# Moving the quarter sums of the last down-projection from GpSimd to VectorE

## The chip, the cores and the metric

The kernel runs on one core of a Trainium2 chip. The metric is device time in microseconds (us) of one execution. A core has TensorE (PE: matrix products; loading a weight tile is shown as PEld), VectorE (DVE), ScalarE (ACT), GpSimd (POOL) and SyncE (SP, whose queue issues all DMAs here). Each engine works through its own instructions in order and waits on semaphores for the others.

## The reference, cut to what matters

One layer of a transformer-like trunk over 1024 latent tokens with 256 context tokens, all in float32 and `D_MODEL = 1024`, `D_FF = 2816`: a half-weighted SwiGLU feed-forward, two kinds of attention merged by gates, and a second half-weighted SwiGLU feed-forward. The change lies in the second feed-forward, the last of the layer:

```python
def _swiglu(h, w1, w3, w2):
    return (jax.nn.silu(h @ w1) * (h @ w3)) @ w2
...
        x = _residual(x, _swiglu(_modnorm(x, g[4], m[6], m[7]), ffn2_w1[l], ffn2_w3[l], ffn2_w2[l]),
                      g[5], m[8], HALF_STEP)
```

`_residual` normalises the rows of its second argument, scales them by `g[5]` and the adaLN gate `m[8]`, and adds them to `x`.

## The kernel before

**Products.** Every float32 matrix is split into a high part that TensorE takes exactly and a low part, the remainder. `split` (line 202) does it: ScalarE copies the source to the high part with rounding, VectorE subtracts the high part from the source for the low part. Three matmuls per tile (high x high, high x low, low x high) give the product (`mm3`; all matmuls are recorded at line 153). Calls on VectorE, ScalarE and GpSimd that go through a helper show line 120, DMAs of SP's queue line 132.

**Seven products instead of eight.** Both projections of the feed-forward cut their matrices into 2 x 2 quarters and use a Strassen-Winograd scheme: seven products of quarters or of sums of quarters. The sums are made ahead of the products.

**Up-projection.** `units2` holds 22 units, two for each of the NP = 11 pairs of feature tiles: one for `w1`, one for `w3`. A unit's products are steps of 12 matmuls; the steps that remain in this stage are named p6, p5, p7, p3, p4 (units that were begun earlier, 14 of the 22) or first, p6, second, p5, p7, p3, p4. Each step's result is read out of its PSUM bank by VectorE. When p4 of a pair's `w3` unit is out, the four gated quarters a11, a12, a21, a22 of that pair (128 x 512 each) are complete, and `Gated.sums` (line 719) makes from them s1 = a21 + a22, s3 = a11 - a21, s2 = s1 - a11 and s4 = a12 - s2, on GpSimd, all four at that point. They go to DRAM; `store` puts a DMA off by a number of steps (4 here). For the pairs begun early, a11 comes back from DRAM beforehand.

**Last stage.** `Quarters` (line 804) is the down-projection: 7 x 11 = 77 steps, numbered 0 to 76, seven quarter products of 11 steps each in the order of `ORDER`:

```python
        ORDER = (("a11", "b11"), ("a12", "b21"), ("s1", "t1"), ("s4", "b22"), ("s2", "t2"), ("s3", "t3"), ("a22", "t4"))
        BANKS = (("s", "s", "s", "m"), ("m", "m", "v", "v"))
```

The left factors are read back from DRAM (`load_a`), the right ones are quarters b11 ... b22 of the weight `ffn2_w2` (`load_b`) or their differences t1 = b12 - b11, t2 = b22 - t1, t3 = b22 - b12, t4 = b21 - t2. `Quarters.sum` (line 842) makes those in place, per pair, on GpSimd: 44 in all. A step multiplies four row tiles into four PSUM banks; after the last step of a quarter product, `out` (line 873) adds the banks to the result `ys`, on ScalarE for the first two products (steps 10 and 21) and on VectorE after that (steps 32, 43, 54, 65, 76). Products 0 and 1, 2 and 3, and 4 to 6 go on accumulating in the same banks, so steps 11, 33, 55 and 66 wait until the banks have been read.

**The order around it.** `Plan` is a list of main steps (TensorE's work with what reads it) and, by step, of side work; `run` records, per step, the main function, its side work in the order in which it was planned, and then the stores that are due. So each engine's order is written out by hand. `Quarters.plan` (line 889) places the left factor's load 7 steps ahead of its use, both splits 3 steps ahead, b11 and b21 7 steps ahead of theirs, b12 from step -1 on, b22 from step 14 on (one pair per step each), and the sums of pair p at steps 9 + p (t1), 26 + p (t2 and t3) and 37 + p (t4). In a step, the split comes ahead of a sum.

Two other things share the stage. The rows of adaLN modulation 8 are computed by VectorE in steps 12 to 38: 16 multiply-adds of 128 x 512 (`ada_steps`, line 2236), and some small matmuls on TensorE. And `done2` (line 2196) makes the residual of row tiles 0 to 3 in steps 55 to 62: a load of `x` and a multiplication in one step, a multiply-add of 128 x 1024 and the store of the output in the next; the last four row tiles follow in halves at the end. Splits, sums and results use the buffer pools "t" (20 of 128 x 512), "u" (24 of 128 x 1024) and "v" (16 of 128 x 1024).

Of the kernel before, what the change touches and what calls it, by code (L numbers as in the profile page):

```python
# [12 lines left out]
ALU = mybir.AluOpType  # L13
# [17 lines left out]
NP = NF // 2  # L31
# [12 lines left out]
def hybrid_block(ctx: ExitStack, tc: tile.TileContext, a: dict, out: bass.AP):  # L44
# [31 lines left out]
    def T2(dt=F32, n=512):  # L76
        return pools["t"].tile([P, n], dt, tag="t", name=nm("t"))
# [10 lines left out]
    def PB(tag):  # L88
        return ps.tile([P, 512], F32, tag=tag, name=nm("b" + tag), bufs=PBUFS[tag])
# [41 lines left out]
    def put(dst, src):  # L131
        return pin(nc.sync.dma_start(dst, src))  # L132

    def store(dst, src, n=2):

        if clock[0] is None:
            return put(dst, src)
        waiting.append((clock[0] + n, dst, src))

    def flush(before=None):  # L140
        while waiting and (before is None or waiting[0][0] <= before):
            put(*waiting.pop(0)[1:])

    deferred = []

    def later(f):
# [3 lines left out]
    vec, act, pool = Engine(nc.vector), Engine(nc.scalar), Engine(nc.gpsimd)  # L150
# [12 lines left out]
    class Plan:  # L163
# [14 lines left out]
        def run(self):  # L178
            for i, f in enumerate(self.main):
                clock[0] = i  # L180
                f()
                for g in self.side.pop(i, ()):
                    g()
                while deferred:
                    deferred.pop(0)()
                flush(i)
            assert not self.side
            clock[0] = None
            flush()
# [229 lines left out]
    class Planes:  # L419
# [52 lines left out]
        def sums(self):  # L472
            def parts(name, src):
                us = self.us[name] = [[], []]

                def one(x):
                    for hl in range(2):
                        us[hl].append(U(F32R, "u" if (name, x, hl) == self.keys.get("u") else self.keys[name]))
                    split_to(us[0][x], us[1][x], src()[x])
                    if x:  # L480
                        self.f[name] = [[half(us[hl], k) for hl in range(2)] for k in range(4)]
                return [lambda x=x: one(x) for x in range(2)]

            t11, t12, t21, t22 = [lambda o=o, s=s: getattr(self, s)[o:o + 2] for s, o in
                                  (("t1", 0), ("t1", 2), ("t2", 0), ("t2", 2))]

            def op(eng, out, x, y, o):
                return [lambda i=i: eng.tensor_tensor(out()[i], x()[i], y()[i], op=o) for i in range(2)]

            return (op(vec, t22, t22, t21, ALU.add) + parts("s1", t22) + op(vec, t21, t11, t21, ALU.subtract)  # L490
                    + op(vec, t22, t22, t11, ALU.subtract) + parts("s2", t22)
                    + op(vec, t12, t12, t22, ALU.subtract) + parts("s3", t21) + parts("s4", t12))

    class Unit:
# [32 lines left out]
        def sum(self, i):  # L527

            if i == 1:
                self.t = []  # L530
            q = {f"{r}{c}": self.r[c - 1][:, (r - 1) * 512:r * 512] for r in (1, 2) for c in (1, 2)}
            x, y = {1: ("12", "11"), 2: ("22", 0), 3: ("22", "12"), 4: ("21", 1)}[i]
            t = T2()
            vec.tensor_tensor(t, q[x], q[y] if isinstance(y, str) else self.t[y], op=ALU.subtract)
            self.t.append(t)
# [86 lines left out]
    def plan_leads(plan, units, n, ahead=0):  # L622

        at = len(plan.main)
        for x in range(0, n, 2):
            two = units[x:x + 2]
            o = at + 2 * x
            if x > ahead:
                plan.spread([lambda u=u: u.load(0) for u in two], max(at, o - 8), max(at, o - 8) + 2)
                plan.spread([lambda u=u, n=n: u.split(n) for n in ("11", "21") for u in two], o - 4, o)  # L630
        plan.step(*lead_main(units[:n]))

    def plan_rest(plan, units):

        for i, u in enumerate(units):
            o = len(plan.main)
            e = plan.step(*u.rest())
            at = lambda n: o + u.names.index(n)
            for n, f in (u.within() if i else []) + (units[i + 1].before() if i + 1 < len(units) else []):
                plan.spread([f], at(n), at(n) + 1)  # L640
            if i + 2 < len(units):
                plan.spread([lambda v=units[i + 2], x=x: v.load(x) for x in (2, 0, 1)], e - 3, e)

    def plan_first_rest(plan, units, early, first, last):
        plan.spread([lambda x=x: units[0].load(x) for x in range(2)], early, early + 1)
        plan.spread([lambda i=i: units[0].sum(i) for i in range(1, 5)], early + 2, early + 4)
        plan.spread(units[0].all_steps(), first, last)
        plan.spread([lambda: units[0].load(2)] + [lambda x=x: units[1].load(x) for x in (2, 0, 1)], last - 2, last)
# [51 lines left out]
    class Gated:  # L700
# [18 lines left out]
        def sums(self, p):  # L719
            a11, a12, a21, a22 = [self.t.pop(n) for n in ("a11", "a12", "a21", "a22")]  # L720
            s1, s4 = T2(), T2()
            pool.tensor_tensor(s1, a21, a22, op=ALU.add)
            pool.tensor_tensor(a21, a11, a21, op=ALU.subtract)
            pool.tensor_tensor(a11, s1, a11, op=ALU.subtract)
            pool.tensor_tensor(s4, a12, a11, op=ALU.subtract)
            for n, x in (("s1", s1), ("s3", a21), ("s2", a11), ("s4", s4)):
                store(self.d[n, p], x, 4)

    def up_units(h, w1, w3, gd):

# [73 lines left out]
    class Quarters:  # L804
# [37 lines left out]
        def sum(self, name, p):  # L842
            out, x, y = {"t1": ("t1", "b12", "b11"), "t3": ("t3", "b22", "b12"),
                         "t2": ("t2", "b22", "t1"), "t4": ("t4", "b21", "t2")}[name]
            pool.tensor_tensor(self.slot(out, p), self.slot(x, p), self.slot(y, p), op=ALU.subtract)

        def banks(self, x):
            self.pb = [PB(t) for t in self.BANKS[x]]
# [40 lines left out]
        def plan(self, plan, ahead=3, loads=4):  # L889

            o = len(plan.main)
            at = lambda n: o + n
            for n in range(self.n):
                plan.spread([lambda n=n: self.load_a(n)], at(n) - ahead - loads, at(n) - ahead - loads + 1)
                x = min(at(n) - ahead, at(self.n - self.LAST) - 1)
                plan.spread([lambda n=n: self.split(n)], x, x + 1)
                plan.step(lambda n=n: self.step(n))
            for p in range(NP):
                for name, first in (("b11", 0), ("b21", NP), ("b12", 6), ("b22", NP + 10)):
                    x = at(first + p) - ahead - loads  # L900
                    plan.spread([lambda name=name, p=p: self.load_b(name, p)], x, x + 1)
                for name, x in (("t1", NP - 2 + p), ("t3", 2 * NP + 4 + p), ("t2", 2 * NP + 4 + p), ("t4", 3 * NP + 4 + p)):
                    plan.spread([lambda name=name, p=p: self.sum(name, p)], at(x), at(x) + 1)
            return o

# [45 lines left out]
    first = [PB("s") for _ in range(3)]  # L951
# [211 lines left out]
    for i, d in enumerate(downs):  # L1163
# [6 lines left out]
        else:  # L1170
            order = ([None] * 4 + list(range(10)) if i == len(downs) - 2 else
                     [0, 1, 2, 3, 4, None, 5, None, 6, None, 7, None, None, 8, 9])
            for t in order:
                if t is None:
                    f, x = ups.pop(0)
# [8 lines left out]
        if i < len(downs) - 2:  # L1184
            n = downs[i + 1]
            plan.spread([lambda n=n: n.loads(n.fs[0])], o, o + 1)
            plan.spread(n.steps(), o + 3, e)
        elif not last:
            n = downs[i + 1]
# [78 lines left out]
    def emit_cq(i, ci, x, bank):  # L1268

        t, q = x, T2()  # L1270
        if bank:
            t = T2()
            act.copy(t, x)
        act.activation(q, t, AF.Square)
        if ci in sq:
            vec.tensor_tensor(sq[ci], sq[ci], q, op=ALU.add)
        else:
            sq[ci] = q
        store(cqx[i, :, ci * 512:(ci + 1) * 512], t)
# [22 lines left out]
    for p in range(3):  # L1302
        punits.append(Unit(h2, [cq_src(2 * p), cq_src(2 * p + 1)],
                           lambda i, ci, x, bank, p=p: emit_cq(2 * p + i, ci, x, bank)))
# [227 lines left out]
    def tiles_of(ci):  # L1532
        return range(CHUNKS[ci][0] // P, sum(CHUNKS[ci]) // P)
# [199 lines left out]
    def head_out(pv, n, h, hi, lo, shape):  # L1733
# [20 lines left out]
        nc.gpsimd.tensor_tensor(lo[b:b + 64], o, f32(hi[b:b + 64]), op=ALU.subtract)  # L1754

    sums, held = {}, [None]

    def wide(n):
# [384 lines left out]
    def chain2(t):  # L2143
        made = []

        def run(x):
            if not made:
                made.extend(residual_steps(y2[t], x1s[t * P:(t + 1) * P, :], lambda: g5row[0], True, ready[t // 4],
                                           after=lambda: store(x2s[t * P:(t + 1) * P, :], y2[t], 1)))
            made[x]()  # L2150
        return [lambda x=x: run(x) for x in range(5)]
# [177 lines left out]
```

## Time and profile before

| | us |
|---|---|
| median of 3 runs | 2626.81 |
| lowest, highest | 2623.81, 2628.51 |
| the profiled execution | 2623.75 |
| its span in the profile | 2622.0 |
| TensorE busy | 2577.2 (98%) |
| VectorE busy | 1891.3 (72%) |
| ScalarE busy | 1190.2 (45%) |
| GpSimd busy | 371.9 (14%) |

How to read it: the profile is one execution, taken by the hardware profiler. A row of a group gives line, engine, operation, output<-inputs by the program's names (xu, xv and t are tiles of the pools u, v, t; bs, bm, bv are PSUM banks; d is a tensor in DRAM), the tile's shape, the count, then busy time in us and the mean of one in ns, and last how long the engine sat idle before such instructions and what ended that. In the timeline a row is start, duration, engine and operation, with the wait before it in brackets; rows of equal kind in a run are merged (x9). Matmuls are pipelined and their ends are modelled, so intervals between starts are used for TensorE. "PEclk" is the clock that TensorE was granted, as a share of full speed. GpSimd's spans are rough.

### The profile page before, as it was taken

Reading aid. Unit: us, or ns where it says so; the run is one execution under the profiler, and the core shown is the slowest. Engines: PE = TensorE matmul, PEld = TensorE weight load, DVE = VectorE, ACT = ScalarE, POOL = GpSimd, SP = SyncE. Lnnn points to the kernel's source line nnn. Section 1 sums busy time; section 2 is a strip of 40 time slices with the busy share of each in tenths; the row PEclk is TensorE's granted clock in tenths of the full one; section 3 lists DMA queues with packets and bytes.
Section 4 is the critical chain, followed back from the end, with each engine's and each line's share of the span. In section 5 each row is a group of like instructions: output and inputs, shape, how many; then the busy total and the mean of one; then the engine's idle time right before and its main releaser. Section 6 shows DMA issues by size and latency. Waiting matters only on the chain. (4 is left out here: it accounts for less than half of the span.)

```text
span 2622.0 us, 38011 instructions
## 1 busy us (share of the span) xinstructions
PE 2577.2 (98%) x13596; PEld 2191.1 (84%) x13596; DVE 1891.3 (72%) x3448; ACT 1190.2 (45%) x2282; POOL 371.9 (14%) x456
## 2 busy tenths in 40 slices
PE   8999999999999999999999999999999999999898
PEld 6888888888888788889889999987788888888687
DVE  4778876588776676774469988887545788778867
ACT  6622233522223763433438988772265322324344
POOL 1000000000000400001004422220030121114613
PEclk9999999999999999999999999999999999999999
DMA  8444433444433665745978722216235454238414
GB/s 307 164 157 144 149 110 123 158 162 157 158 135 105 219 235 185 241 149 180 299 287 294 221 75 76 68 49 217 84 131 170 165 176 146 100 117 302 162 58 173
DMA packets 213501, 433.30 MB, mean 165 GB/s; under 512 B 26880, under 2 KB 68032, under 8 KB 213312
## 3 DMA queue, kind: packets, MB, share of 16 engines
q1 hardware_dynamic: 213312, 430.87, 49.1%
q8 instruction: 107, 1.75, 0.3%
q14 instruction: 82, 0.67, 0.1%
HBM read 318.78 MB, written 112.00 MB: 164 GB/s over the span
## 5 line engine op out<-in xcount | busy, mean ns | idle before, releaser
L153 PE MATMUL bm<-xu,xu 128*128 128x512 f32 (+1 forms) x1980 | 469.6, 388 | 0.6 <-DVE xu L120 0.3
L153 PEld LDWEIGHTS bm<-xu,xu 128*128 128x128 f32 x1980 | 363.4, 188 | 73.9 <-ACT t L120 1.4
L153 PE MATMUL bs<-xv,xu 128*128 128x512 f32 x1488 | 357.3, 389 | 0.3 <-DVE t L120 0.3
L153 PE MATMUL bv<-xv,xu 128*128 128x512 f32 x1342 | 335.4, 389 | 0.0
L153 PE MATMUL bs<-xu,xu 128*128 128x512 f32 (+1 forms) x1404 | 334.0, 384 | 0.0
L153 PEld LDWEIGHTS bs<-xv,xu 128*128 128x128 f32 x1488 | 279.2, 188 | 58.5 <-issue 0.7
L120 ACT CAST xu<-t 128x512 fp32r<-128x512 f32 x260 | 158.4, 616 | 352.6 <-DVE t L120 352.1
L153 PEld LDWEIGHTS bs<-xu,xu 128*128 128x128 f32 x1404 | 258.0, 188 | 52.0 <-issue 0.8
L153 PEld LDWEIGHTS bv<-xv,xu 128*128 128x128 f32 x1342 | 251.9, 188 | 52.3
L120 DVE TENSOR_TENSOR xu<-t,xu 128x512 fp32r<-128x512 f32 x260 | 181.6, 700 | 127.5 <-ACT xu L120 127.5
L120 POOL TENSOR_SCALAR st<-st 128x1 f32<-128x1 f32 (+1 forms) x66 | 42.6, 646 | 1413.2 <-ACT t L120 1402.8
L120 DVE TENSOR_TENSOR xu<-xu,xu 128x512 fp32r<-128x512 f32 (+1 forms) x212 | 161.3, 766 | 65.9 <-ACT xu L120 65.5
L153 PE MATMUL bs<-w,w 96*128 96x512 f32 (+3 forms) x832 | 206.4, 367 | 2.4 <-DVE st L1798 2.0
L120 DVE TENSOR_TENSOR xu<-xv,xu 128x512 fp32r<-128x512 f32 (+4 forms) x196 | 141.4, 744 | 42.0 <-ACT xu L120 38.8
L153 PE MATMUL bm<-t,xu 128*128 128x256 f32 (+1 forms) x1272 | 165.3, 287 | 0.6 <-ACT t L120 0.4
L153 PEld LDWEIGHTS bm<-t,xu 128*128 128x128 f32 x1272 | 160.7, 191 | 6.0 <-ACT t L120 0.8
L120 ACT ACTIVATE t<-t 128x512 f32<-128x512 f32 (+1 forms) x94 | 57.3, 610 | 226.7 <-DVE t L120 211.7
L153 PE MATMUL bv<-t,w 128*128 128x256 f32 x896 | 151.5, 288 | 2.8 <-DVE t L1936 2.0
L153 PEld LDWEIGHTS bv<-t,w 128*128 128x128 f32 x896 | 132.8, 189 | 18.6 <-DVE t L1936 6.9
L120 ACT CAST xu<-xu 128x512 fp32r<-128x512 f32 (+1 forms) x212 | 130.2, 624 | 14.9 <-DMA xu<-in_f1w 7.8
L153 PEld LDWEIGHTS bs<-w,w 96*128 96x128 f32 (+1 forms) x832 | 123.6, 190 | 10.8 <-DVE st L1798 3.5
L1936 DVE TENSOR_TENSOR t<-bm,t 128x512 fp32r<-128x512 f32 x160 | 110.0, 688 | 27.7 <-ACT t L1935 27.2
(227 smaller groups left out, 4304.6 us busy)
## 6 DMA issues: line engine op xcount, KB each, us to landing
d<-t SPq DMA_DIRECT2D x305, 256.0 KB, 2.7
t<-d SPq DMA_DIRECT2D x160, 256.0 KB, 3.8
xv<-in_f1w SPq DMA_DIRECT2D x64, 512.0 KB, 3.6
xu<-in_f1w SPq DMA_DIRECT2D x61, 512.0 KB, 3.8
xu<-in_f2w SPq DMA_DIRECT2D x58, 512.0 KB, 3.7
t<-in_wada SPq DMA_DIRECT2D x112, 256.0 KB, 3.9
xv<-d SPq DMA_DIRECT2D x40, 512.0 KB, 6.0
xu<-in_winT SPq DMA_DIRECT2D x38, 512.0 KB, 4.8
```

Source lines behind the costliest of these rows:

```text
L120: return lambda *x, **y: pin(f(*x, **y))
L153: return pin(nc.tensor.matmul(o, s, m, start=start, stop=stop, skip_group_check=open_group[0]))
L1936: nc.vector.tensor_tensor(t[1], pb, f32(t[0]), op=ALU.subtract)
```

## The change

`Plan.run` gets a list `owed` and, at the end of each step's side work, runs one entry of it. `Gated.sums` puts its four sums there, each with its store, on VectorE: s1 in the step of p4, the others in the three steps after it, and each store two steps after its sum. `Quarters.sum` runs on VectorE. In `Quarters.plan` b12 is loaded three steps later and b22 five steps later, and the sums of pair p stand at steps 4 + 3p/2 (t1), 23 + 3p/2 (t2), 40 + p (t3) and 52 + p (t4), rounded down. The operands, results and number of all operations and DMAs stay.

```diff
+    owed = []
     deferred = []
...
                 while deferred:
                     deferred.pop(0)()
+                if owed:
+                    owed.pop(0)()
                 flush(i)
...
             a11, a12, a21, a22 = [self.t.pop(n) for n in ("a11", "a12", "a21", "a22")]
             s1, s4 = T2(), T2()
-            pool.tensor_tensor(s1, a21, a22, op=ALU.add)
-            pool.tensor_tensor(a21, a11, a21, op=ALU.subtract)
-            pool.tensor_tensor(a11, s1, a11, op=ALU.subtract)
-            pool.tensor_tensor(s4, a12, a11, op=ALU.subtract)
-            for n, x in (("s1", s1), ("s3", a21), ("s2", a11), ("s4", s4)):
-                store(self.d[n, p], x, 4)
+
+            def one(name, out, x, y, op):
+                vec.tensor_tensor(out, x, y, op=op)
+                store(self.d[name, p], out)
+
+            for x in (("s1", s1, a21, a22, ALU.add), ("s3", a21, a11, a21, ALU.subtract),
+                      ("s2", a11, s1, a11, ALU.subtract), ("s4", s4, a12, a11, ALU.subtract)):
+                owed.append(lambda x=x: one(*x))
...
-            pool.tensor_tensor(self.slot(out, p), self.slot(x, p), self.slot(y, p), op=ALU.subtract)
+            vec.tensor_tensor(self.slot(out, p), self.slot(x, p), self.slot(y, p), op=ALU.subtract)
...
-                for name, first in (("b11", 0), ("b21", NP), ("b12", 6), ("b22", NP + 10)):
+                for name, first in (("b11", 0), ("b21", NP), ("b12", 9), ("b22", 2 * NP + 4)):
                     x = at(first + p) - ahead - loads
                     plan.spread([lambda name=name, p=p: self.load_b(name, p)], x, x + 1)
-                for name, x in (("t1", NP - 2 + p), ("t3", 2 * NP + 4 + p), ("t2", 2 * NP + 4 + p), ("t4", 3 * NP + 4 + p)):
+                for name, x in (("t1", 4 + 3 * p // 2), ("t2", 2 * NP + 1 + 3 * p // 2), ("t3", 4 * NP - 4 + p), ("t4", 5 * NP - 3 + p)):
                     plan.spread([lambda name=name, p=p: self.sum(name, p)], at(x), at(x) + 1)
```

## The prediction

> **What bounds the kernel now.** I read the page's busy shares by slice, then busy time in windows cut at the last two stages, then who TensorE waits for, then its timeline.
>
> ```profile
> span 2622.0 us, 38011 instructions
> ...
> PE   8999999999999999999999999999999999999898
> ...
> POOL 1000000000000400001004422220030121114613
> ```
>
> A slice is 65.6 us. TensorE is full nearly everywhere; the slice from 2425 to 2491 is one of the few at 8, and there GpSimd shows a 6.
>
> ```profile
> core 0: us, PE busy (x) PEld busy (x) DVE busy (x) ACT busy (x) POOL busy (x), PEclk, DMA share, GB/s
> 2047.40:2383.40 336.00, 336.00 (x1484) 278.29 (x1484) 251.96 (x352) 103.30 (x181) 63.52 (x40) 1.00 0.41 139
> ...
> 2458.60:2489.80 31.20, 18.33 (x73) 12.86 (x72) 31.20 (x24) 7.96 (x14) 27.43 (x17) 0.96 0.37 110
> 2489.80:2506.60 16.80, 16.76 (x71) 13.10 (x72) 15.03 (x18) 4.58 (x8) 10.21 (x7) 0.87 0.50 146
> 2506.60:2583.60 77.00, 77.00 (x345) 63.66 (x343) 48.51 (x71) 38.40 (x68) 7.23 (x8) 1.00 0.25 87
> 2583.60:2614.90 31.30, 30.32 (x133) 24.70 (x132) 22.83 (x37) 13.41 (x31) 12.48 (x7) 1.00 0.39 145
> ```
>
> The up-projection (2047 to 2383) has no idle TensorE. In the middle of the last stage VectorE is busy without a gap (31.20 of 31.20 us), GpSimd nearly so, and TensorE works 18.33 us. Once GpSimd's sums are done, VectorE falls to 48.51 of 77 us and TensorE is full. So TensorE sets the time, except where VectorE does:
>
> ```profile
> PE bm L153 <- DVE xv L120: 12.9, 7, 6.9
> PE bs L153 <- DVE xv L120: 1.9, 4, 1.0
> ```
>
> In the last two stages TensorE waits for nothing but VectorE's low halves and additions (xv). The loss itself comes from TensorE's timeline:
>
> ```profile
> 2383.36 2.20 PE L153 MATMUL bs<-xv,xv 128*128 128x512 f32 x9
> ...
> 2458.64 0.39 PE L153 MATMUL bm<-xv,xv 128*128 128x512 f32 x1
> ...
> 2489.84 2.90 PE L153 MATMUL bm<-xv,xv 128*128 128x512 f32 x6 [6.89 <-DVE xv L120]
> ...
> 2506.56 1.52 PE L153 MATMUL bm<-xv,xv 128*128 128x512 f32 x6
> ...
> 2578.18 2.20 PE L153 MATMUL bs<-xv,xv 128*128 128x512 f32 x9
> ...
> 2580.90 2.20 PE L153 MATMUL bs<-xv,xv 128*128 128x512 f32 x9
> ...
> 2584.76 2.29 PE L153 MATMUL bs<-xv,xv 128*128 128x512 f32 x9 [0.98 <-DVE xv L120]
> ...
> 2612.05 2.88 PE L153 MATMUL bm<-xv,xv 128*128 128x512 f32 x12
> ```
>
> A step of 12 matmuls takes 2580.90 - 2578.18 = 2.72 us undisturbed, so 77 steps need 209.4. They ran from 2383.36 to 2612.05 + 2.88 = 2614.93: 231.6. Of the 22.1 us between, about 2 are small matmuls that stay (8 + 8 + 2 of them):
>
> ```profile
> L156 PE MATMUL bs<-ident,st 128*128 128x128 f32 x8 | 1.0, 272 | 0.0
> L153 PE MATMUL bs<-t,strip 128*32 128x256 f32 x8 | 0.6, 391 | 0.0
> L156 PE MATMUL bs<-ident,t 128*128 128x128 f32 x2 | 0.4, 272 | 0.0
> ```
>
> The losses, by step numbers of the last stage: before step 27 (due 2383.36 + 27 x 2.72 = 2456.80, there at 2458.64) 1.84; from there to step 33 (2489.84) 31.20 - 6 x 2.72 = 14.88; to step 38 (2506.56) 16.72 - 13.60 = 3.12, of which 1.0 is small matmuls: 2.1; to step 66 (2584.76) 78.20 - 76.16 = 2.04, less 1.0: about 1.1. Together 20 us.
>
> **The change part by part.** *The 44 sums leave GpSimd.* The reason for the stall is in VectorE's groups, first between 2383.4 and 2506.6, then between 2506.6 and 2583.6, where GpSimd has no sums:
>
> ```profile
> L120 DVE TENSOR_TENSOR xv<-xu,xv 128x512 fp32r<-128x512 f32 x40 | 53.4, 1336 | 0.0
> L120 DVE TENSOR_TENSOR xv<-t,xv 128x512 fp32r<-128x512 f32 x39 | 45.4, 1165 | 12.4 <-ACT xv L120 12.4
> ...
> L120 DVE TENSOR_TENSOR xv<-t,xv 128x512 fp32r<-128x512 f32 x27 | 18.6, 689 | 19.9 <-ACT xv L120 19.9
> L120 DVE TENSOR_TENSOR xv<-xu,xv 128x512 fp32r<-128x512 f32 x27 | 18.5, 686 | 0.0
> L120 DVE SCALAR_TENSOR_TENSOR xu<-xu,st,xu 128x1024 f32<-128x1024 f32 x4 | 5.1, 1285 | 6.6 <-DMA xu<-d 6.6
> ```
>
> One and the same subtraction averages 1165 to 1336 ns beside GpSimd's sums and 686 to 689 ns without. The single ones:
>
> ```profile
> 2459.78 0.74 DVE L120 SCALAR_TENSOR_TENSOR t<-t,sc,t 128x512 f32<-128x512 f32 x1
> 2460.44 1.78 DVE L120 TENSOR_TENSOR xv<-t,xv 128x512 fp32r<-128x512 f32 x1
> 2462.14 1.77 DVE L120 TENSOR_TENSOR xv<-xu,xv 128x512 fp32r<-128x512 f32 x1
> 2463.83 0.74 DVE L120 SCALAR_TENSOR_TENSOR t<-t,sc,t 128x512 f32<-128x512 f32 x1
> ```
>
> Two subtractions at 1.77 and an adaLN multiply-add make a cycle of 2463.83 - 2459.78 = 4.05 us, against TensorE's 2.72: 1.33 lost per step over some six steps, then step 33, which first needs the additions of step 32 out of its banks. Without GpSimd the cycle is 2 x 0.69 + 0.74 = 2.12 us, and a sum at 0.69 makes 2.81; but there are two sums in three steps here (t1, t2) and 16 adaLN operations in 26 steps, so a mean of 1.38 + 0.46 + 0.46 = 2.30 us. That fits into 2.72, and the splits stand three steps ahead. So 14.88 and the 2.1 behind it go. For the first 1.84 the bounds are 0 and 1.84: the splits are faster, but the loads of these steps are tight, too. I take 0.5, since the waits were for VectorE.
>
> *The price on VectorE.* 44 x 0.69 = 30 us in the last stage, behind each step's split and hidden as above. If that cover is gone they cost up to 30 us, a sum at a time.
>
> *Four sums per pair in the up-projection.* The same trade, from VectorE's groups between 2047.4 and 2383.4 and GpSimd's until 2506.6:
>
> ```profile
> L120 DVE TENSOR_TENSOR xu<-xu,xu 128x512 fp32r<-128x512 f32 x37 | 40.7, 1100 | 0.0
> L120 DVE TENSOR_TENSOR t<-xu,t 128x512 f32<-128x512 f32 x42 | 33.8, 806 | 0.0
> L120 DVE TENSOR_TENSOR t<-xu,xu 128x512 f32<-128x512 f32 x21 | 20.9, 997 | 0.0
> ...
> L120 POOL TENSOR_TENSOR t<-t,t 128x512 f32<-128x512 f32 x44 | 70.0, 1591 | 354.3 <-DVE t L120 217.0 <-ACT xu L120 113.6 <-issue 21.1
> L120 POOL TENSOR_TENSOR xu<-xu,xu 128x512 f32<-128x512 f32 x33 | 54.7, 1683 | 32.4 <-DVE xv L120 27.9 <-DMA xu<-in_f2w 4.5
> ```
>
> At 0.69 each these three groups would be 37 x 0.41 + 42 x 0.12 + 21 x 0.31 = 27 us shorter; 44 new sums are 30. VectorE's load stays (251.96 of 336 us), one sum per step instead of stalls in lumps, and each split is made two steps (5.4 us) ahead. Cost 0; bounds 0 and 30 us, all sums on the path.
>
> *New waits on VectorE.* Its queue is in order: behind a sum stand the next step's splits, and TensorE waits for those. t1 of pair 0 comes two steps after its load of b12, t2 four after b22; GpSimd waited 4.5 us for such a load in all. Two steps plus the three of the splits are 13.6 us of cover: cost 0, upper bound 4.5. SP's stores of the last pair's sums stand at steps 1 to 4 instead of 3, each holding the loads queued behind it until VectorE has that sum; s4 comes after four splits and three sums, about 12 x 0.69 = 8.3 us after the up-projection's end, the time that GpSimd needed for four sums (4 x 1.59 = 6.4) plus 2: inside the 0.5. Bytes and DMA count stay; b12 and b22 are loaded three and five steps later, which spreads the start. ScalarE and TensorE keep their order.
>
> *What is late next.* Steps 54 to 62 also hold the residuals of the first four row tiles, and t4 now comes there, one per step:
>
> ```profile
> 2559.25 1.28 DVE L120 SCALAR_TENSOR_TENSOR xu<-xu,st,xu 128x1024 f32<-128x1024 f32 x1
> 2566.11 1.29 DVE L120 SCALAR_TENSOR_TENSOR xu<-xu,st,xu 128x1024 f32<-128x1024 f32 x1 [2.03 <-DMA xu<-d]
> ...
> 2580.32 1.29 DVE L120 SCALAR_TENSOR_TENSOR xu<-xu,st,xu 128x1024 f32<-128x1024 f32 x1 [2.58 <-DMA xu<-d]
> 2583.93 1.88 DVE L120 TENSOR_TENSOR xv<-xv,bs 128x512 f32<-128x512 f32 x3
> ```
>
> These four form a chain: the store of one holds SP's next residual load, for which the next one waits; some 7 us a turn, against 5.44 for two steps. At its end the additions of step 65 are late, and step 66 waits for their banks. Two sums more per turn (1.4) fit into the 2.0 to 2.6 us that VectorE sits waiting. But three (t4 of pairs 2 to 4) come ahead of the first link, which no wait hides: 3 x 0.69 = 2.1. The 1.1 before step 66 becomes 3.2.
>
> The rule that bears on 3.2: the Trainium skill, "TensorE: Matmul & The Clock Gate" (Why this matters for your kernels), warns of TensorE gaps over about 3 us, after which it runs at half clock. The trace agrees for the gap of 6.89: six matmuls in 2.90 us instead of 1.52, clock 0.87. By the rule a gap of 3.2 would be paid again; it is a rival below.
>
> The Trainium skill's "Perfetto Trace Analysis" (Optimizing Scalar/DVE Operations) says that offloading from a saturated VectorE even to GpSimd may make sense, but adds that they share an SBUF read port. The first half speaks against this change, and by it the last stage would grow by up to 30 us; the rows (1.77 beside GpSimd, 0.69 without) bear out the second half.
>
> *Sum.* 20 - 0.5 - 3.2 = 16.5 us. The profiled execution took 2623.75 (1.75 around its span), 3.06 less than the median of 2626.81: 2607.2 against its own time, 2610.3 against the median. What the measurement can tell from no change is 0.2%, 5.3 us.
>
> **The rivals.**
> 1. *Step 66's gap costs clock, too.* After the long gap steps 33 to 37 lost 2.1; the same again gives 2612.4. For it: 3.2 lies just above the rule's bound. Against: the gap of 0.98 left the clock at 1.00 (last window above).
> 2. *Two thirds of the gain: the sums wait for loads or the tight start stays.* VectorE inherits GpSimd's 4.5 us behind b12 and the 1.84 stays, in front of splits with no lead left: 16.5 - 4.5 - 1.3 = 10.7 gained, 2616.
> 3. *It does nothing:* 1.77 us is not GpSimd's doing (DMA, ScalarE), or VectorE stays the pace through the added sums. 2627. Against: VectorE's rate turns exactly when GpSimd ends.
> 4. *Slower: the up-projection breaks.* A sum there waits on VectorE for a late a11 reload or for a buffer that a store still reads; what it holds up are TensorE's bank readouts. It decides once such a wait exceeds the two steps of lead, 5.44 us; then a pair loses about the sums' own 4 x 0.69 = 2.8 us, 11 pairs 30 us: 2610 + 30 = 2640. Against: GpSimd's group shows no DMA wait for these operands, and TensorE had no gap in 336 us although VectorE suffered lumps of about the same size.
>
> **How the numbers follow.** Forecast 0.63 (own range 2606.6, no gap at all, to 2613), rival 1 0.10, rival 2 0.15, rival 3 0.06, rival 4 0.06. Range 2603 to 2617: below by the 3 us that executions before differ among themselves, above past rivals 1 and 2. It leaves out rivals 3 and 4 and some of 2. Faster 0.88, same 0.06, slower 0.06.
>
> **What would show it.** Right: in the last stage VectorE's subtractions all at 0.69; steps 27 to 38 at 2.72 with clock 1.00; the wait before step 33 gone and the one before step 66 near 3 us; VectorE's total busy time about unchanged; GpSimd's sums gone from its groups. Wrong: gaps of TensorE in the up-projection, VectorE waiting for loads of in_f2w, or matmul steps longer than 2.72 with 0.69 us subtractions.

## The result and the profile after

| | median, us | lowest to highest | runs |
|---|---|---|---|
| before, same chip | 2627.07 | 2623.81 to 2628.51 | 4 |
| changed | 2612.03 | 2609.17 to 2613.24 | 4 |

The ratio is 0.9943, with a 95% interval from 0.9926 to 0.9960: faster by 15.0 us, where 16.5 were forecast. The profiled execution took 2611.61 us. In the changed kernel the recorded lines stand one lower, so matmuls show L154; in variants of the kernel before they show L153.

First the page of the changed kernel: span, busy time by engine, and the slices of TensorE and GpSimd.

```profile
span 2609.8 us, 37912 instructions
...
PE 2576.4 (99%) x13596; PEld 2194.1 (84%) x13596; DVE 1869.2 (72%) x3536; ACT 1189.7 (46%) x2282; POOL 229.4 (9%) x368
...
PE   8999999999999999999999999999999999999998
...
POOL 1000000000000400001003522221021000000003
```

The slice that stood at 8 (2425 to 2491 us) is a 9, and GpSimd has nothing to do there. GpSimd lost 371.9 - 229.4 = 142.5 us. VectorE took over its 88 sums and is nevertheless busy 22 us less than the 1891.3 of before. The same windows as before, for the changed kernel:

```profile
2047.40:2383.40 336.00, 336.00 (x1484) 278.19 (x1484) 245.68 (x390) 102.55 (x180) 0.00 (x0) 1.00 0.42 139
2383.40:2458.60 75.20, 75.20 (x333) 62.28 (x332) 54.51 (x90) 30.69 (x54) 0.00 (x0) 1.00 0.89 320
2458.60:2489.80 31.20, 31.20 (x144) 25.22 (x143) 26.01 (x44) 12.57 (x22) 0.00 (x0) 1.00 0.56 166
2489.80:2506.60 16.80, 16.80 (x80) 13.99 (x79) 9.57 (x17) 7.83 (x14) 0.00 (x0) 1.00 0.34 104
2506.60:2583.60 77.00, 73.97 (x320) 60.74 (x319) 66.50 (x101) 38.43 (x72) 18.72 (x12) 0.98 0.33 120
```

In the third row TensorE (second number) was busy 18.33 us and is now full, while VectorE (fourth) does its splits and its sums in 26.01 of 31.20 us where it had no pause before. The clock of 0.96 and 0.87 in the third and fourth windows is 1.00. In the last window it is the other way: TensorE, full before, loses 3.03 us, and the clock reads 0.98. TensorE's timeline of the changed kernel (start, duration) shows the only place:

```profile
2386.31 2.20 PE L154 MATMUL bs<-xv,xv 128*128 128x512 f32 x9
...
2565.05 2.23 PE L154 MATMUL bs<-xv,xv 128*128 128x512 f32 x9
2567.12 0.84 PE L154 MATMUL bm<-xv,xv 128*128 128x512 f32 x3
2570.99 3.06 PE L154 MATMUL bs<-xv,xv 128*128 128x512 f32 x9 [3.03 <-DVE xv L120]
...
2578.14 2.20 PE L154 MATMUL bs<-xv,xv 128*128 128x512 f32 x9
...
2599.90 2.88 PE L154 MATMUL bm<-xv,xv 128*128 128x512 f32 x12
```

Step 0 starts at 2386.31 and step 65 at 2565.05: 178.74 us, of which 65 x 2.72 = 176.80 are steps and the rest is the 2 us of small matmuls. So nothing is lost for 65 steps. Step 66 was due at 2565.05 + 2.72 = 2567.77 and comes 3.22 us late. Then the two steps 66 and 67 take 2578.14 - 2570.99 = 7.15 us instead of 5.44: nine matmuls last 3.06 instead of 2.20, so the clock was down, at a cost of 1.71 us. The whole stage takes 2599.90 + 2.88 - 2386.31 = 216.47 us, against 231.57 before: 15.1 shorter, which is the whole gain of 15.0. (The profiled execution came into the last stage 2.95 us later than that of before, out of stages that the change doesn't touch. There its clock fell to half twice, for 3.41 us each time, and that of before not at all; the last section shows one such place. In the runs whose up-projection has no gap of TensorE, the stage begins at 2383.4 to 2383.7 us with no such stretch ahead of it, at 2384.9 to 2385.3 with one, at 2385.2 to 2386.3 with two and at 2388.2 with three. So variants are compared by the length of this stage as well as by their times.)

VectorE's timeline of the changed kernel, first in the stretch that lost most before, then along the residual chain ahead of step 66: the additions of product 4, the four residuals, the additions of step 65.

```profile
2460.60 0.69 DVE L120 TENSOR_TENSOR xv<-t,xv 128x512 fp32r<-128x512 f32 x1
2461.21 0.69 DVE L120 TENSOR_TENSOR xv<-xu,xv 128x512 fp32r<-128x512 f32 x1
2461.82 0.69 DVE L120 TENSOR_TENSOR xu<-xu,xu 128x512 f32<-128x512 f32 x1
2462.42 0.75 DVE L120 SCALAR_TENSOR_TENSOR t<-t,sc,t 128x512 f32<-128x512 f32 x1
2463.33 0.69 DVE L120 TENSOR_TENSOR xv<-t,xv 128x512 fp32r<-128x512 f32 x1 [0.16 <-ACT xv L120]
...
2536.01 2.05 DVE L120 TENSOR_TENSOR xv<-xv,bs 128x512 f32<-128x512 f32 x3 [0.85 <-PE bs L154]
...
2545.21 1.28 DVE L120 SCALAR_TENSOR_TENSOR xu<-xu,st,xu 128x1024 f32<-128x1024 f32 x1
...
2552.17 1.28 DVE L120 SCALAR_TENSOR_TENSOR xu<-xu,st,xu 128x1024 f32<-128x1024 f32 x1 [0.94 <-DMA xu<-d]
...
2559.62 1.28 DVE L120 SCALAR_TENSOR_TENSOR xu<-xu,st,xu 128x1024 f32<-128x1024 f32 x1 [1.40 <-DMA xu<-d]
...
2566.55 1.28 DVE L120 SCALAR_TENSOR_TENSOR xu<-xu,st,xu 128x1024 f32<-128x1024 f32 x1 [0.89 <-DMA xu<-d]
...
2570.16 1.88 DVE L120 TENSOR_TENSOR xv<-xv,bs 128x512 f32<-128x512 f32 x3
```

The two splits of a step, a sum of the weight and an adaLN multiply-add stand in 2.73 us (2463.33, the next split, less 2460.60). Before, the two splits and the multiply-add alone took 4.05.

In the chain the turns are still about 7 us (6.96, 7.45, 6.93). The waits in them have shrunk from 2.0 to 2.6 us to 0.9 to 1.4: two sums a turn went into them. The last additions begin at 2570.16, 2.4 us after step 66 was due.

### The profile page after: what moved, and what is told of

Read it like the earlier page. It is cut to its first block, busy times and chain, and to the rows that moved or that the text cites. A ratio compares the mean times of both kernels' runs of the same rounds, so it can differ in the third digit from the quotient of the medians.

```text
span 2609.8 us, 37912 instructions
## 1 busy us (share of the span) xinstructions
PE 2576.4 (99%) x13596; PEld 2194.1 (84%) x13596; DVE 1869.2 (72%) x3536; ACT 1189.7 (46%) x2282; POOL 229.4 (9%) x368
## 4 chain that ended last, share of the span: by engine, by line
PE 55%; issue 32%; DVE 6%; ACT 4%; DMA 1%; POOL 1%; SPq 0%; DVEq 0%; ACTq 0%; POOLq 0%
PE bs L154 24%; PE bm L154 16%; PE bv L154 12%; PE bm L157 2%; ACT xu L1914 1%; DVE xu L1778 1%; DVE xv L120 1%; DVE t L1941 1%; ACT t L1940 1%; DVE xu L120 1%; PE bs L157 1%; DVE t L120 1%; POOL st L120 1%; ACT t L1914 0%; ACT t L1754 0%
## 5 line engine op out<-in xcount | busy, mean ns | idle before, releaser
L154 PE MATMUL bm<-xu,xu 128*128 128x512 f32 (+1 forms) x1980 | 469.6, 388 | 1.1 <-ACT t L120 0.8
L154 PEld LDWEIGHTS bm<-xu,xu 128*128 128x128 f32 x1980 | 363.4, 188 | 74.5 <-ACT t L120 2.1
L154 PE MATMUL bs<-xv,xu 128*128 128x512 f32 x1488 | 357.3, 389 | 0.3 <-DVE t L120 0.3
L154 PE MATMUL bv<-xv,xu 128*128 128x512 f32 x1342 | 335.4, 389 | 0.0
L154 PE MATMUL bs<-xu,xu 128*128 128x512 f32 (+1 forms) x1404 | 334.0, 384 | 0.0
L154 PEld LDWEIGHTS bs<-xv,xu 128*128 128x128 f32 x1488 | 279.2, 188 | 58.5 <-issue 0.7
L154 PEld LDWEIGHTS bs<-xu,xu 128*128 128x128 f32 x1404 | 258.0, 188 | 52.0 <-issue 0.8
L154 PEld LDWEIGHTS bv<-xv,xu 128*128 128x128 f32 x1342 | 251.9, 188 | 52.3
L120 DVE TENSOR_TENSOR xu<-xu,xu 128x512 fp32r<-128x512 f32 (+2 forms) x245 | 168.5, 692 | 66.2 <-ACT xu L120 64.6
L154 PE MATMUL bs<-w,w 96*128 96x512 f32 (+3 forms) x832 | 206.8, 367 | 2.4 <-DVE st L1803 1.9
L154 PE MATMUL bm<-t,xu 128*128 128x256 f32 (+1 forms) x1272 | 165.3, 287 | 0.6 <-ACT t L120 0.4
L154 PEld LDWEIGHTS bm<-t,xu 128*128 128x128 f32 x1272 | 160.7, 191 | 6.0 <-ACT t L120 0.8
L120 DVE TENSOR_TENSOR t<-t,t 128x512 f32<-128x512 f32 (+2 forms) x196 | 125.2, 639 | 45.6 <-ACT t L120 42.0
L154 PE MATMUL bv<-t,w 128*128 128x256 f32 x896 | 152.0, 289 | 2.6 <-DVE t L1941 1.9
L154 PEld LDWEIGHTS bv<-t,w 128*128 128x128 f32 x896 | 133.2, 190 | 18.3 <-DVE t L1941 6.8
L154 PEld LDWEIGHTS bs<-w,w 96*128 96x128 f32 (+1 forms) x832 | 124.1, 191 | 10.8 <-DVE st L1803 3.3
```

Of the source, the lines that this page charges most:

```text
L120: return lambda *x, **y: pin(f(*x, **y))
L154: return pin(nc.tensor.matmul(o, s, m, start=start, stop=stop, skip_group_check=open_group[0]))
```

## The experiments

Stage is the time from the first matmul of the last stage to the end of the last. Ratios stand against the kernel before on the same chip.

| run | median, us | ratio, 95% interval | stage, us |
|---|---|---|---|
| before | 2627.07 | | 231.57 |
| changed | 2612.03 | 0.9943 [0.9926, 0.9960] | 216.47 |
| e1 weight's sums only | 2610.73 | 0.9943 [0.9928, 0.9958] | 216.74 |
| e2 up-projection's sums only | 2625.13 | 0.9998 [0.9988, 1.0007] | 230.92 |
| e3 new places, on GpSimd | 2619.88 | 0.9976 [0.9966, 0.9987] | 225.30 |
| e4 VectorE, old places | 2618.74 | 0.9969 [0.9959, 0.9980] | 213.99 |
| e5 t3, t4 earlier | 2607.93 | 0.9928 [0.9916, 0.9941] | 212.71 |
| e6 stores later | 2606.03 | 0.9922 [0.9909, 0.9936] | 212.17 |
| e7 e5 and e6 | 2606.37 | 0.9922 [0.9909, 0.9934] | 211.54 |
| e8 fills on GpSimd | 2607.74 | 0.9928 [0.9914, 0.9941] | 213.08 |
| e9 weight's sums on VectorE at old steps | 2607.73 | 0.9926 [0.9913, 0.9938] | 213.14 |
| e10 copies on GpSimd | 2607.72 | 0.9929 [0.9916, 0.9943] | 213.78 |
| e11 four sums at once | 2620.93 | 0.9979 [0.9970, 0.9988] | 216.45 |
| e12 e9 and e6 | 2606.75 | 0.9924 [0.9910, 0.9937] | 212.07 |

Against the expectations below, the medians of e1, e5, e6, e7 and e9 lie 0.1 to 1.3 us under the range of their theory, and those of e2, e3 and e4 lie between theory and rival. Each trace is of one execution.

### Which part carries the gain: e1 to e4

e1 is the change without its up-projection half (`Gated.sums` and `run` as before); e2 is the up-projection half alone.

> Only the 44 sums of the weight as in the change (VectorE, new steps); the 44 of the up-projection stay on GpSimd. Theory (the stall is the last stage's VectorE beside GpSimd's weight sums): 2612 to 2614 us, nearly the whole gain; the first steps may keep up to 0.5 us of their 1.84, since GpSimd still makes the last pair's four sums there. Rival (the up-projection's sums carry a part): 2616 or more.

> Only the 44 sums of the up-projection as in the change; the weight's sums stay on GpSimd at their old steps. Theory: 2626 to 2627 us, TensorE's 14.9 us between steps 27 and 33 unchanged. Rival (the up-projection's sums carry a part): 2623 or less; if four sums per pair on VectorE were a burden, over 2628.

e1 has the change's ratio and, within 0.3 us, its stage, with one wait of 3.3 us before step 66. e2 can't be told from the kernel before, and its stage shows the old wait of 6.9 us. So the gain is the weight's sums; moving the sums of the gated quarters alone changes the time by nothing that can be told.

Both halves end one loss, though. Step 27, which came 1.84 us late before, is on time in e1 and 0.03 us late in e2. GpSimd's timeline of the kernel before shows what stood there:

```profile
2385.11 6.72 POOL L120 TENSOR_TENSOR t<-t,t 128x512 f32<-128x512 f32 x4 [30.64 <-DVE t L120]
2391.79 11.93 POOL L120 TENSOR_TENSOR xu<-xu 128x512 f32<-128x512 f32 x7
```

These are the last pair's four sums and, straight behind them, seven of the weight's. The seven are planned for steps 9 to 15, but GpSimd had nothing else to do and began them in step 3. So each of VectorE's subtractions from 2385.50 to 2402.50 took 1.77 or 1.78 us. Either half of the change takes one of the two groups away, and the loss goes. e2 gives most of it back: steps 33 to 37 lose 2.8 us instead of 2.1, and step 66 comes 1.6 us late instead of 1.1.

e3 and e4 take the two parts of the move apart: places, and engine.

```diff
 e3, against the kernel before
-("b12", 6), ("b22", NP + 10)
+("b12", 9), ("b22", 2 * NP + 4)
...
-("t1", NP - 2 + p), ("t3", 2 * NP + 4 + p), ("t2", 2 * NP + 4 + p), ("t4", 3 * NP + 4 + p)
+("t1", 4 + 3 * p // 2), ("t2", 2 * NP + 1 + 3 * p // 2), ("t3", 4 * NP - 4 + p), ("t4", 5 * NP - 3 + p)
 e4, against the kernel before: in sums and sum
-pool.tensor_tensor(
+vec.tensor_tensor(
```

> All sums stay on GpSimd, but the weight's sums and loads stand at the new steps. Theory A (the engine does it): wherever GpSimd sums, VectorE's subtractions stay at 1.77 us and the stall before step 33 stays in most part: 2622 or more. Theory B (the places do it: one sum in one and a half steps costs VectorE 0.73 us per step, 2.57 in all, which fits in 2.72): no stall up to step 54, then three sums at 1.1 instead of 0.69 ahead of the residual chain, a gap before step 66 of 4.4 us with the slow clock behind it: 2614 to 2617.

> All 88 sums on VectorE, at the old steps (four at once per pair in the up-projection, t2 and t3 of a pair in the same step). Theory A (the engine does it): in steps 26 to 36 VectorE has 1.38 + 1.38 + 0.46 = 3.2 us for 2.72, 5.5 us late in all against a lead of three steps, a loss of 0 to 5 us there; the gap before step 66 stays at 1.1: 2608 to 2613. Theory B (the places do it): 2620 or more.

e3 fell between both expectations. With at most two sums in three steps and no t3 between, TensorE loses nothing up to step 32, although the sums are on GpSimd. What it keeps are mainly two gaps, each with a slow clock behind it (0.8 us more go between steps 55 and 65); TensorE's timeline of e3:

```profile
2482.29 2.90 PE L153 MATMUL bm<-xv,xv 128*128 128x512 f32 x6 [6.04 <-DVE xv L120]
2484.99 2.65 PE L153 MATMUL bv<-xv,xv 128*128 128x512 f32 x6
2487.48 1.53 PE L153 MATMUL bm<-xv,xv 128*128 128x512 f32 x6
...
2580.09 3.63 PE L153 MATMUL bs<-xv,xv 128*128 128x512 f32 x9 [2.66 <-DVE xv L120]
...
2584.25 2.22 PE L153 MATMUL bs<-xv,xv 128*128 128x512 f32 x9
```

Spreading alone is worth 231.57 - 225.30 = 6.3 us of the stage. The engine alone (e4) is worth more than the change: 231.57 - 213.99 = 17.6, with gaps of 0.25 us before step 33 and 1.43 before step 66, and no slow clock behind them. But e4 comes into the last stage at 2398.26, 12 us later than the change. Of these, 10.2 come from the up-projection, where its four sums of a pair stand in one place: the 125 steps (1500 matmuls) ahead of the last stage take 350.2 us, against 340.0 in the change and before. TensorE's timeline of e4 there has such a gap at ten of the eleven pairs, six times like this:

```profile
2078.82 3.01 PE L153 MATMUL bs<-xv,xu 128*128 128x512 f32 x12 [0.71 <-DVE t L120]
...
2107.02 3.00 PE L153 MATMUL bs<-xv,xu 128*128 128x512 f32 x12 [0.71 <-DVE t L120]
```

### How much room the up-projection has: e9 and e11

Either e4's loss comes from those four sums in one place, or from the weight's loads and sums at their old steps. e9 is the change with the weight's loads and sums at the old steps (e3's diff the other way), on VectorE. e11 is the change with the four sums made at once:

```diff
 e11, against the change
-                owed.append(lambda x=x: one(*x))
+                one(*x)
```

> The up-projection as in the change (one sum per step on VectorE), the weight's sums on VectorE at their old steps with the old loads. Theory (engine in the last stage, spreading in the up-projection): TensorE has no gap in the up-projection, and the last stage takes the 214.0 us of the kernel with all sums on VectorE at the old steps, with gaps near 0.5 before step 33 and 1.5 before step 66: 2609 to 2611 us, 2 to 3 us below the change. Rival (the new steps of the weight's sums are needed): over 2613.

> The change, with the four sums of a pair made on VectorE all at once where p4 is read out, instead of one per step; their stores as in the change, two steps behind. Theory (VectorE's queue in the up-projection has less room than four sums at one place, 4 x 0.69 = 2.8 us; each such pair costs TensorE some 0.7 to 1 us, the last stage is as in the change): the last stage begins 9 to 13 us later than with the change and takes the change's 216.5; 2621 to 2625 us, about as before the change. Rival (what was lost with all sums at their old steps came from the weight's sums or loads, not from these four): no gaps in the up-projection, 2610 to 2613 us.

e9 has no gap in the up-projection and the short stage, 213.14. So the new steps for the weight's sums, which the change brought along, made its stage 3.3 us longer, not shorter. e11 has the change's stage, 216.45, but starts it at 2395.58. Its 125 steps ahead of that take 350.3 us, 10.3 more than in the change; it arrives only 9.3 us later because its execution had one stretch at half clock less before them. Its median missed the expected 2621 to 2625 by 0.1 us, on the side of a smaller loss. TensorE's timeline of e11, and behind it VectorE's, at the first such pair:

```profile
2072.47 2.88 PE L154 MATMUL bv<-xv,xu 128*128 128x512 f32 x12
2076.07 3.00 PE L154 MATMUL bs<-xv,xu 128*128 128x512 f32 x12 [0.71 <-DVE t L120]
2078.91 1.75 PE L154 MATMUL bv<-xv,xu 128*128 128x512 f32 x7
```

```profile
2071.12 3.59 DVE L120 TENSOR_TENSOR t<-t,t 128x512 f32<-128x512 f32 x5
2074.63 0.68 DVE L120 TENSOR_TENSOR xu<-t,xu 128x512 fp32r<-128x512 f32 x1
2075.24 0.68 DVE L120 TENSOR_TENSOR t<-bs,t 128x512 f32<-128x512 f32 x1
```

Five operations in a row: the gating product of a quarter and the four sums, 3.59 us. Behind them stands the split and then the readout of a bank (t<-bs), which ends at 2075.92; TensorE's step needs that bank, was due at 2072.47 + 2.72 = 2075.19, and starts at 2076.07. So a lump of 4 x 0.69 = 2.8 us is 0.9 us too long, and the room at this place is about 1.9 us by this estimate, not the two steps (5.4 us) by which the splits lead. One sum per step is what keeps the second half of the change free.

### What made the subtractions slow: e8 and e10

The sums of the weight on GpSimd are replaced by a fill, which reads nothing, or by a copy, which reads one tile instead of two. Places and everything else are those of the kernel before.

```diff
 e8 and e10, against the kernel before
-pool.tensor_tensor(self.slot(out, p), self.slot(x, p), self.slot(y, p), op=ALU.subtract)
+pool.memset(self.slot(out, p), 0.0)
...
+pool.tensor_copy(self.slot(out, p), self.slot(x, p))
```

> The kernel before, with GpSimd filling the 44 destinations of the weight's sums with zeros instead of subtracting; the products with t1 to t4 are therefore left out of the result (they are multiplied as zeros). Same engine, same places, same size of output, but nothing read from SBUF. Theory (GpSimd's reading of two tiles slows VectorE's two-input operations): VectorE's subtractions in the last stage all at 0.69 us, no gap before step 33, the stage at 213 to 215 us as with the sums on VectorE at the old steps, so 2607 to 2611 us. Rival (any work of GpSimd on SBUF slows them): subtractions beside a fill still at 1.7 to 1.8 us; if the fills last as long as the sums (1.6 us) the time stays at 2622 to 2627.

> The kernel before, with GpSimd copying the first operand of each of the 44 sums of the weight instead of subtracting the second, so the subtraction is left out of the result. GpSimd reads one tile and writes one. Theory (it is GpSimd's reading at all that makes VectorE's two-input operations alternate with it): the subtractions beside a copy are slower than 0.69 us, between 1.0 and 1.8, and the time lies between 2612 and 2627. Rival (only a second input does it): 0.69 throughout, and 2607 to 2611 us.

VectorE's and GpSimd's timeline of e8, then the same of e10, both in the stretch that lost most before:

```profile
2452.07 1.00 POOL L120 MEMSET xu<- 128x512 f32 x2 [0.87 <-DVE xv L120]
2452.58 0.69 DVE L120 TENSOR_TENSOR xv<-t,xv 128x512 fp32r<-128x512 f32 x1
2453.18 0.69 DVE L120 TENSOR_TENSOR xv<-xu,xv 128x512 fp32r<-128x512 f32 x1
```

```profile
2450.16 2.10 POOL L120 COPY xu<-xu 128x512 f32<-128x512 f32 x2 [0.60 <-DVE xv L120]
2450.68 1.10 DVE L120 TENSOR_TENSOR xv<-t,xv 128x512 fp32r<-128x512 f32 x1
2451.70 1.09 DVE L120 TENSOR_TENSOR xv<-xu,xv 128x512 fp32r<-128x512 f32 x1
2452.72 0.74 DVE L120 SCALAR_TENSOR_TENSOR t<-t,sc,t 128x512 f32<-128x512 f32 x1
2452.86 2.09 POOL L120 COPY xu<-xu 128x512 f32<-128x512 f32 x2 [0.60 <-DVE xv L120]
2453.38 1.09 DVE L120 TENSOR_TENSOR xv<-t,xv 128x512 fp32r<-128x512 f32 x1
```

The subtraction takes 0.69 us beside a fill, 1.10 beside a copy and 1.77 beside a subtraction. So it is what GpSimd reads that VectorE pays for. With fills in the places of before, the stage is 213.08 us without a gap before step 33: neither the places nor GpSimd's writes made the stall. The Trainium skill, "SBUF — State Buffer" (SBUF: two separate sides), says that a VectorE instruction with two inputs in SBUF contends with a GpSimd instruction that reads SBUF and not with one that only writes; the 0.69 beside fills and the 1.10 and 1.77 beside reads agree.

The time of e10 came out as its rival had it, though, with the theory's slow subtractions. The cycle says why: from 2450.68 to 2453.38 it is 2.70 us, just under TensorE's 2.72. Slower subtractions cost next to nothing until their cycle passes the step (e10's stage is 0.7 us longer than e8's, all of it lost before step 33); at 4.05 they cost 1.33 a step.

### What is left before step 66: e5, e6, e7 and e12

```diff
 e5, against the change
-("t3", 4 * NP - 4 + p), ("t4", 5 * NP - 3 + p)
+("t3", 39 + 14 * p // 11), ("t4", 40 + 13 * p // 11)
 e6, against the change: in done2
-store(out[t * P:(t + 1) * P, :], z, 0)
+store(out[t * P:(t + 1) * P, :], z, 3)
```

e5 takes t4 out of the steps of the residuals. e6 puts the store of each finished row tile off by three steps, so that it no longer holds SP's next residual load. e7 does both; e12 is e9 with e6's edit.

> The change, with t3 and t4 made in steps 39 to 51 instead of 40 to 62. Theory (three sums ahead of the residual chain made the gap before step 66): that gap falls from 3.2 to 1.1 to 1.5 us and the slow clock behind it goes; the last stage 213.0 to 213.5 instead of 216.5 us, the time 2608 to 2609.5. Rival (the chain of residual loads alone makes the gap): gap 3 us, 2612.

> The change, with the first four output stores put off by three steps, so that SP issues the next residual load without waiting for VectorE. Theory (store, load and multiply-add form a chain of 7 us a turn): VectorE no longer waits for these loads, its work from the additions of step 54 to those of step 65 takes 30.9 us for 29.9, the gap before step 66 goes to under 0.5 with no slow clock: last stage 211.5 to 212.5, the time 2607 to 2608. Rival (VectorE has too much work there, with or without the chain): gap of 2 us or more, over 2610.

> Both: t3 and t4 in steps 39 to 51, and the output stores three steps later. Theory: no gap of TensorE is left in the last stage, which takes 77 x 2.72 = 209.4 us and 2.2 for small matmuls: 211.6; the time 2606.5 to 2607.5, no better than the later stores alone by more than 0.5.

> The two best edits together: sums of the gated quarters one per step as in the change, the weight's sums on VectorE at the steps and loads of before, and the store of each finished row tile put off by three steps. Theory (what is left in the last stage is the chain of residual loads behind the stores, 0.8 us before step 66, and 0.25 before step 33): the gap before step 66 goes, the one before step 33 stays, stage 211.5 to 212.5 us; 2604.5 to 2607 us. Rival (with either edit alone the gap is already so small that the other gives nothing that can be measured): 2606 to 2608 us.

VectorE's timeline of e5 and, behind it, that of e6, from the first residual to the last:

```profile
2542.42 1.28 DVE L120 SCALAR_TENSOR_TENSOR xu<-xu,st,xu 128x1024 f32<-128x1024 f32 x1
...
2563.39 1.28 DVE L120 SCALAR_TENSOR_TENSOR xu<-xu,st,xu 128x1024 f32<-128x1024 f32 x1 [2.13 <-DMA xu<-d]
```

```profile
2543.90 1.28 DVE L120 SCALAR_TENSOR_TENSOR xu<-xu,st,xu 128x1024 f32<-128x1024 f32 x1
2550.65 1.28 DVE L120 SCALAR_TENSOR_TENSOR xu<-xu,st,xu 128x1024 f32<-128x1024 f32 x1 [0.72 <-POOL st L120]
2556.62 1.27 DVE L120 SCALAR_TENSOR_TENSOR xu<-xu,st,xu 128x1024 f32<-128x1024 f32 x1
2562.56 1.27 DVE L120 SCALAR_TENSOR_TENSOR xu<-xu,st,xu 128x1024 f32<-128x1024 f32 x1
```

In e5 the turns stay at 7 us (20.97 for three, waits of 2.13 for the load are back), but the chain starts earlier: 2542.42 is 157.10 us after that run's first step (2385.32), in the change it was 2545.21 - 2386.31 = 158.90. That is 1.80 us, near the 2.1 of three sums, and with the 0.37 of shorter turns the chain ends 2.17 earlier; TensorE idles 0.88 us there instead of 3.03. In e6 the start stays and the chain itself breaks: no residual waits for a load, the last two turns are 5.97 and 5.94, and the idle time is 0.36 us. Both lose the slow clock with the gap. With both (e7) TensorE waits for nothing in either projection, and the stage is 211.54, which is 77 x 2.72 + 2 and cannot be shortened by waits any more. e12's stage is as expected, its time in both expectations.

These are versions that beat the kernel before and the change: medians of 2606.0 to 2607.9, 19 to 21 us under the 2626.2 to 2626.8 of before on their chips, against 15.0. They were not timed on one chip with the change, and the intervals of the ratios overlap with its own; what separates them is the stage, 3.3 to 4.9 us shorter, and that the highest of their 25 runs, 2608.81, lies under the lowest of the change's four, 2609.17. Among e5, e6, e7, e9 and e12 no order is shown.

## Why the prediction was right

*What bounds the kernel.* The 20 us of loss in the last stage were the right account: e7, in which no wait is left, has a stage 231.57 - 211.54 = 20.0 us shorter.

*The sums leave GpSimd.* Right, and the reason holds: steps 27 to 38 run at 2.72 us and clock 1.00. The 0.5 left for the start was too careful; no step up to 65 lost anything. What had cost 1.84 there was GpSimd again, with sums of both kinds in a row (e1 and e2), and not the loads that the prediction named beside it: e2 leaves these as they were. e3 adds what the prediction didn't separate: fewer sums per step on GpSimd would have ended the loss before step 33 too, but not the wait at that step.

*The price on VectorE.* 30 us in the last stage and 30 in the up-projection, both hidden, as said. In the up-projection's window VectorE has 390 - 352 = 38 operations more, 26.2 us at 0.69, and is busy 245.68 instead of 251.96: the others became 32.5 us shorter, where 27 were worked out from three groups.

*The up-projection.* The cost of 0 was right, the cover named for it was wrong. The prediction took the two steps of lead of the splits, 5.4 us. Its rival 4 did name the readouts of banks, but let them decide only beyond those 5.4 us. e11 puts the limit at 1.9 us of VectorE's queue in one place, since it is not a split but a bank's readout that comes late; the change passes it because it makes its sums one at a time. That rival's price was too high: e11 lost 10.3 us, not 30.

*Loads.* VectorE waits for no load of `in_f2w` in the last stage, as taken; rival 2's first half did not come, and its second, the tight start, did not either.

*Step 66.* The wait was forecast at 3.2 and is 3.22 us. The 2.1 us that it added to the 1.1 of before are not quite the three sums, though: the first residual stands 1.81 us later against step 65 (2565.05 - 2545.21 = 19.84 ahead of it, before 2580.90 - 2559.25 = 21.65), and the chain takes 0.27 us more (21.34, before 21.07). That the sum fits so closely is luck. That three sums of t4 ahead of the first residual make most of it is shown by e5, that the chain of loads behind stores is what carries it to step 66 by e6.

*The mis-sized terms.* The sum was 20 - 0.5 - 3.2 = 16.5. The runs have 20 - 0 - 3.2 - 1.7 = 15.1. The start was over-priced by 0.5, and rival 1 came about together with the forecast: the gap cost 1.7 us of clock besides, priced there at 2.1. The measured 15.0 lie nearer to rival 1's 14.4 than to the forecast's 16.5; that they lie near both is partly luck, because the two errors go opposite ways and partly cancel. Weighing the gap of 0.98, which left the clock alone, against a gap of 3.2 was the weak step: it speaks only for gaps near its own length. The rule of the Trainium skill, "TensorE: Matmul & The Clock Gate" (Why this matters for your kernels), that gaps over about 3 us cost the clock, gave the right answer here: 3.03 us idle, nine matmuls in 3.06 instead of 2.20.

*Rival 3*, that GpSimd isn't the cause, is out by e8 and e10, in which nothing but GpSimd's instruction was replaced.

## What to carry to other kernels

Look for the slow instruction before asking which engine is full: VectorE was busy without a pause, and taking on 88 more operations made it less busy, because its own had been stretched by what GpSimd read. Compare the cycle of an engine's work per step with the step of the engine that sets the time: beneath it next to nothing is gained or lost, above it every step pays. And place moved work in an in-order queue one piece at a time, asking at each place what stands directly behind it; the same four sums were free when spread and cost 10 us in one lump.

## What the runs showed of the hardware

The clock fell after gaps shorter than expected: 3.03 us idle cost 1.7 us in the change, and in e3 2.66 us idle was followed by nine matmuls in 3.63 us, so that the step took 2584.25 - 2580.09 = 4.16 instead of 2.72. A gap of 1.43 (e4) left the matmuls after it at 2.20 to 2.29. But no limit of length can be read from this, because the same shorter idle time was paid in one execution and not in another. Far ahead of the change, TensorE idles 1.87 to 1.88 us in every run. Its row and a window behind it, first of the changed kernel, then of the kernel before:

```profile
1383.51 2.20 PE L154 MATMUL bs<-w,w 128*128 128x256 f32 x8 [1.87 <-DVE st L1803]
1384.50:1387.80 3.30, 3.30 (x16) 3.20 (x15) 2.42 (x13) 0.37 (x1) 0.00 (x0) 0.50 0.99 348
```

```profile
1381.77 1.79 PE L153 MATMUL bs<-w,w 128*128 128x256 f32 x8 [1.88 <-DVE st L1798]
1382.00:1385.40 3.40, 3.40 (x25) 3.15 (x25) 3.22 (x18) 1.04 (x3) 0.00 (x0) 1.00 0.97 344
```

The clock (third number from the end) is 0.50 in one and 1.00 in the other. Of the fourteen profiled executions, twelve have this stretch of 3.41 us at half clock; that of before and that of e9 have not. What decides is not shown. The Trainium skill, "TensorE: Matmul & The Clock Gate" (Why this matters for your kernels), puts the bound at about 3 us; here shorter gaps were paid for, too, and the measurement decides.

VectorE's subtraction of two tiles has three prices beside GpSimd, 0.69, 1.10 and 1.77 us, by the number of tiles that GpSimd reads (none, one, two). GpSimd's three operations also last differently long (0.50, 1.05 and 1.71 us each beside VectorE); these runs don't separate the length from the number of tiles.
